# Split GELU and multiply in fp32: loads and stores trade queues, GELU in place, one instruction per tile

## The chip, the cores and the metric

The kernel runs on one core of a Trainium2 chip. The metric is the device time of one execution in microseconds (us), as a median over several runs. A profile is one execution, recorded with every instruction and every DMA packet. Its span is a little shorter than the measured time: the profiled execution of the kernel before shows a span of 469.1 us.

## The reference

```python
x: (32, 512, 2048) float32            # 134.22 MB in
x1, x2 = x[..., :1024], x[..., 1024:]
gelu_x1 = 0.5 * x1 * (1 + erf(x1 / np.sqrt(2)))
return (gelu_x1 * x2).astype(np.float32)   # 67.11 MB out
```

## The kernel before

The 16384 rows are cut into 16 tiles of 128 partitions x 8 rows. A tile's load is 8.39 MB, 64 KB a partition; its store is 4.19 MB, 32 KB a partition. There are two input tiles and two output tiles, so a load is two tiles ahead of the compute. ScalarE writes GELU of the left half into the output tile, VectorE multiplies it there by the right half. Middle tiles go in pieces of five and three rows; the first and the last tile in pieces of two, two and four.

```python
def load(i):
    x_tile = xpool.tile([P, R, dim], x.dtype, name="x_tile")      # bufs=2
    ... nc.sync.dma_start(out=x_tile[:, rows, :], in_=x_t[i][:, rows, :])

steps = ((0, 2), (2, 4), (4, 8)) if pieces else ((0, 5), (5, 8))
for lo, hi in steps:
    ... nc.scalar.activation(out=o_tile[:, rows, :], in_=x_tile[:, rows, :half], func=GELU)
    mul = nc.vector.tensor_mul(out=o_tile[:, rows, :], in0=o_tile[:, rows, :],
                               in1=x_tile[:, rows, half:])
...
if not pieces:
    store(nc.sync if i == n_tiles - 2 else nc.scalar, i, o_tile, slice(0, R))
if i + 2 < n_tiles:
    ahead.append(load(i + 2))
```

Because GELU writes the output tile, it waits for two things: the load of its tile and the store of two tiles ago.

## Time and profile before

| | before |
|---|---|
| time, median of 3 runs | 470.53 us (470.52 to 470.63) |
| span of the profile | 469.1 us |
| VectorE busy, ScalarE busy | 140.5 us, 115.5 us |
| mean share of the 16 DMA engines, 1.8 to 468 us | 1.00 |
| one middle tile | 29.05 us |

The prediction below shows the lines that carry this. Two more views are of use later. The first is the table of DMA queues of the kernel before (queue and kind, packets, MB, share of the 16 engines' time). SyncE's queue is q1, ScalarE's is q10.

```profile
q1 hardware_dynamic: 2880, 142.61, 70.4%
q10 hardware_dynamic: 2160, 58.72, 29.0%
```

Time and bytes are in proportion (0.49% per MB on both), so neither queue is the slower one. The second is the timeline at tile 1: start, duration, engine, line, operation.

```profile
60.38 0.36 ACTq L54 DMA_DIRECT2D out_dram<-o_tile  x1
71.58 7.12 ACT L71 ACTIVATE o_tile<-x_tile 128x5120 f32<-128x5120 f32 x2 [17.37 <-DMA out_dram<-o_tile]
```

Tile 1's store is issued at 60.38 us, and the transfers already under way end at about 71.6 us, when the next GELU can start. I call this distance, 11.2 us here, the **lead**: how long before the running transfers land the next ones are queued. In the steady state it is 15.7 us.

### The profile page before, as it was taken

How to read it: one execution, taken by the hardware profiler on the slowest of the kernel's cores; microseconds unless marked ns; L12 is line 12 of the kernel's file. 1: busy time of each engine (PE TensorE's matmuls, PEld its weight loads, DVE VectorE, ACT ScalarE, POOL GpSimd, SP SyncE). 2: the span in 40 equal slices, each digit the busy share in tenths (PEclk: the TensorE clock that was granted, in tenths of full speed). 3: DMA queues.
4: the chain of work that ended last, by engine and by line, in shares of the span. 5: the costliest groups of instructions: out<-in, count | busy, mean ns of one | idle time of the engine just before them, and what ended most of it. 6: DMA issues, size and time to landing. Idle time of an engine off the chain costs nothing.

```text
span 469.1 us, 179 instructions
## 1 busy us (share of the span) xinstructions
DVE 140.5 (30%) x34; ACT 115.5 (25%) x35; POOL 0.2 (0%) x4
## 2 busy tenths in 40 slices
DVE  0330615206051160611506015070250702407042
ACT  1320606041060410605005050050601406014060
POOL 0000000000000000000000000000000000000000
DMA  8999999999999999999999999999999999999998
GB/s 358 447 447 447 414 391 492 402 402 447 492 402 402 447 469 425 402 441 408 492 402 425 425 492 402 402 447 486 408 402 444 455 441 402 441 408 486 408 406 355
DMA packets 5041, 201.34 MB, mean 429 GB/s; under 512 B 560, under 2 KB 560, under 8 KB 560
## 3 DMA queue, kind: packets, MB, share of 16 engines
q1 hardware_dynamic: 2880, 142.61, 70.4%
q10 hardware_dynamic: 2160, 58.72, 29.0%
q14 instruction: 1, 0.01, 0.0%
HBM read 134.22 MB, written 67.11 MB: 429 GB/s over the span
## 4 chain that ended last, share of the span: by engine, by line
DMA 75%; DVE 14%; ACT 8%; ACTq 0%; issue 0%; SPq 0%
DMA out_dram<-o_tile 66%; DVE o_tile L75 14%; DMA x_tile<-in_x_dram 10%; ACT o_tile L71 8%; ACTq L115 0%; SPq L49 0%
## 5 line engine op out<-in xcount | busy, mean ns | idle before, releaser
L75 DVE TENSOR_TENSOR o_tile<-o_tile,x_tile 128x5120 f32<-128x5120 f32 (+3 forms) x34 | 140.5, 4171 | 320.4 <-ACT o_tile L71 320.4
L71 ACT ACTIVATE o_tile<-x_tile 128x5120 f32<-128x5120 f32 (+3 forms) x34 | 114.3, 3407 | 340.1 <-DMA out_dram<-o_tile 302.4
L71 ACT ACT_TABLE_LOAD x1 | 1.3, 1283 | 0.7 <-PEq L104 0.7
L104 POOL MEMSET const-bfloat16-1.0<- 128x1 bf16 x1 | 0.1, 101 | 0.0
L104 POOL MEMSET const-uint8-127<- 128x1 uint8 x1 | 0.1, 101 | 0.0
L104 POOL MEMSET const-float32-0.0<- 128x1 f32 x1 | 0.1, 98 | 0.2 <-issue 0.2
L104 POOL MEMSET const-float32-1.0<- 128x1 f32 x1 | 0.1, 98 | 0.0
## 6 DMA issues: line engine op xcount, KB each, us to landing
out_dram<-o_tile ACTq DMA_DIRECT2D x13, 4096.0 KB, 44.8
x_tile<-in_x_dram SPq DMA_DIRECT2D x2, 4096.0 KB, 16.8
out_dram<-o_tile ACTq DMA_DIRECT2D x2, 2048.0 KB, 34.3
out_dram<-o_tile SPq DMA_DIRECT2D x1, 4096.0 KB, 25.2
out_dram<-o_tile SPq DMA_DIRECT2D x2, 2048.0 KB, 7.5
x_tile<-in_x_dram SPq DMA_DIRECT2D x15, 44.6
```

Source lines behind the costliest of these rows:

```text
L71: nc.scalar.activation(out=o_tile[:, rows, :], in_=x_tile[:, rows, :half], func=GELU)
L75: mul = nc.vector.tensor_mul(out=o_tile[:, rows, :], in0=o_tile[:, rows, :], in1=x_tile[:, rows, half:],)
L104: nc = _bacc.Bacc("TRN2", target_bir_lowering=False, num_devices=1)
```

## The change

The intent is to take ScalarE off the wait for stores: GELU is computed in place in the input tile, and only the multiply needs a free output tile. Loads go out from ScalarE's queue and stores from SyncE's, the middle tiles use one instruction per engine, and waits that others imply are dropped.

```diff
-            dma = nc.sync.dma_start(out=x_tile[:, rows, :], in_=x_t[i][:, rows, :])
+            dma = nc.scalar.dma_start(out=x_tile[:, rows, :], in_=x_t[i][:, rows, :])
...
-        steps = ((0, 2), (2, 4), (4, 8)) if pieces else ((0, 5), (5, 8))
+        steps = ((0, 2), (2, 4), (4, 8)) if pieces else ((0, 8),)
...
-                    out=o_tile[:, rows, :], in_=x_tile[:, rows, :half], func=GELU
+                    out=x_tile[:, rows, :half], in_=x_tile[:, rows, :half], func=GELU
...
-                in0=o_tile[:, rows, :],
+                in0=x_tile[:, rows, :half],
                 in1=x_tile[:, rows, half:],
...
-            for ins in before_gelu[i % 2]:
-                tc.declare_no_dep(mul.ins, ins, reason="ScalarE waited for it")
+            no_wait(mul.ins, loads[i] + x_users[i % 2] + o_users[i % 2])
...
-            store(nc.sync if i == n_tiles - 2 else nc.scalar, i, o_tile, slice(0, R))
+            nc.sync.dma_start(out=o_t[i], in_=o_tile)
```

## The prediction

> **What bounds the kernel now.** I read the page first: the span, the busy shares, the strip of DMA business and the bytes.
>
> ```profile
> span 469.1 us, 179 instructions
> DVE 140.5 (30%) x34; ACT 115.5 (25%) x35; POOL 0.2 (0%) x4
> DMA  8999999999999999999999999999999999999998
> HBM read 134.22 MB, written 67.11 MB: 429 GB/s over the span
> ```
>
> VectorE (DVE) works 30% of the span and ScalarE (ACT) 25%. The DMA strip shows 9 in every slice but the first and the last. That is business, not yet rate, so the second view was the table of busy time by stretch, with cuts at 1.8 us, at 468 us, and around ten periods of the steady state (from one tile's first GELU at 129.49 us to another's at 420.00 us). The columns are the stretch, its length, DVE, ACT and POOL busy, a clock that says nothing here, the mean share of the 16 DMA engines, and GB/s.
>
> ```profile
> 0.00:1.80 1.80, 0.00 (x0) 1.08 (x1) 0.20 (x4) 1.00 0.40 109
> 1.80:468.00 466.20, 140.48 (x34) 114.46 (x35) 0.00 (x0) 1.00 1.00 431
> 468.00:469.10 1.10, 0.00 (x0) 0.00 (x0) 0.00 (x0) 1.00 0.00 0
> 129.49:420.00 290.51, 87.60 (x20) 71.22 (x20) 0.00 (x0) 1.00 1.00 433
> ```
>
> All 16 DMA engines are full, share 1.00, for 466.2 us out of 469.1 (packets are booked at their start, hence some bytes in the first row). The bytes that the reference demands, 134.22 + 67.11 = 201.33 MB, in 466.2 us are 431.9 GB/s. Ten steady tiles take 290.51 us, 29.05 us each; a tile is 8.39 MB in and 4.19 MB out, 12.58 MB, and 12.58 MB / 29.05 us = 433 GB/s. The kernel is bound by the rate of its DMA engines. The span is 1.8 us of start, 466.2 us of transfer and 1.1 us of end.
>
> The chain of waits seems to say otherwise, and was the third view, with the sums of the waits beside it.
>
> ```profile
> DMA out_dram<-o_tile 66%; DVE o_tile L75 14%; DMA x_tile<-in_x_dram 10%; ACT o_tile L71 8%; ACTq L115 0%; SPq L49 0%
> ACT o_tile L71 <- DMA out_dram<-o_tile: 302.4, 14, 22.0
> out_dram<-o_tile ACTq DMA_DIRECT2D x13, 4096.0 KB, 44.8
> x_tile<-in_x_dram SPq DMA_DIRECT2D x15, 44.6
> ```
>
> The chain runs GELU, multiply, store, and back to the GELU two tiles on, which writes the same output buffer; 22% of it is compute, and ScalarE waits 302.4 us for stores, some 22 us for each of 14 tiles. But a store takes 44.8 us from issue to landing although its 4.19 MB need only 9.7 us at 433 GB/s: it waits behind, and shares the engines with, other transfers. A load takes 44.6 us as well. The two, issued together, land together. So a wait for the store is a wait for the DMA engines, and the load that the same GELU needs comes no earlier. One period of the timeline shows the slack:
>
> ```profile
> 390.95 7.12 ACT L71 ACTIVATE o_tile<-x_tile 128x5120 f32<-128x5120 f32 x2 [21.89 <-DMA out_dram<-o_tile]
> 395.45 8.76 DVE L75 TENSOR_TENSOR o_tile<-o_tile,x_tile 128x5120 f32<-128x5120 f32 x2 [20.25 <-ACT o_tile L71]
> 404.24 0.33 SPq L49 DMA_DIRECT2D x_tile<-in_x_dram  x1
> 404.25 0.36 ACTq L54 DMA_DIRECT2D out_dram<-o_tile  x1
> 420.00 7.12 ACT L71 ACTIVATE o_tile<-x_tile 128x5120 f32<-128x5120 f32 x2 [21.93 <-DMA out_dram<-o_tile]
> ```
>
> The new load and store are queued at 404.25 us, 13.3 us after the tile's data were there (390.95). The pair before them keeps the engines busy until about 420.0. The queues are therefore refilled 15.7 us before they would run dry. This lead is the number on which the prediction rests.
>
> **What the Trainium skill says.** "DMA: Bandwidth & Descriptors", section "Issuing engines are not separate DMA queues", says that DMAs issued by different engines share the same 16 DMA engines, and that several issuers save only issue time. The trace agrees: one issue is 0.33 or 0.36 us against 29 us of period. The same page, section "Queues, rings and completion order", says that each DMA engine takes turns between the queues that have work, packet by packet. If a packet is one partition's contiguous piece, 64 KB of a load (8.39 MB / 128) and 32 KB of a store, that gives loads twice the bytes of stores, which fits the equal landing times (44.6 and 44.8 us), whichever queue carries which. Its section "Where 436 GB/s comes from" has a ceiling of 435.2 GB/s; the trace's 433 is 99.5% of it. Fourth, "VectorE: DVE Perf Modes", section "The TRN2 errata — SBUF-src ops pay a fixed extra latency per instruction", has (N+151)/0.96 ns for an fp32 product of two tensors: 5491 ns for 5120 elements, where the trace has 5492.
>
> **The change part by part.** (a) Swapped queues. Loads now leave from ScalarE, stores from SyncE. The build has the three first loads ahead of the activation-table load on ScalarE, so the first transfer starts when it did; an issue there costs 0.36 us instead of 0.33, or 0.03 us once at the start. The table load (1.28 us) moves to about 2 us, while the first data are there only at 12.9 us. No byte and no packet size changes. Sum: 0.0 us.
>
> (b) Whole-tile instructions. The groups by shape give the costs:
>
> ```profile
> L75 DVE TENSOR_TENSOR o_tile<-o_tile,x_tile 128x5120 f32<-128x5120 f32 x14 | 76.9, 5492 | 279.9 <-ACT o_tile L71 279.9
> L71 ACT ACTIVATE o_tile<-x_tile 128x5120 f32<-128x5120 f32 x14 | 62.6, 4469 | 301.2 <-DMA out_dram<-o_tile 280.3 <-DMA x_tile<-in_x_dram 20.9
> L75 DVE TENSOR_TENSOR o_tile<-o_tile,x_tile 128x3072 f32<-128x3072 f32 x14 | 46.9, 3351 | 0.0
> L71 ACT ACTIVATE o_tile<-x_tile 128x3072 f32<-128x3072 f32 x14 | 38.5, 2747 | 0.0
> ```
>
> ScalarE: (4469 - 2747) / 2048 = 0.841 ns an element, so 2747 + 5120 x 0.841 = 7.05 us for 8192. VectorE: (5492 - 3351) / 2048 = 1.045 ns, so 3351 + 5120 x 1.045 = 8.70 us. Fourteen instructions fewer on each engine save 14 x 0.16 us of ScalarE and 14 x 0.14 us of VectorE, both idle most of the time. But nothing overlaps within a tile any more: 7.05 + 8.70 = 15.75 us from data to stored result, where it was 404.25 - 390.95 = 13.3. That is 2.5 us later in each of 14 tiles, 35 us if it were on the path. It is not: the lead falls from 15.7 to 13.2 us and stays far from zero. Sum: 0.0 us.
>
> (c) GELU in place. It no longer waits for the store of two tiles ago; the multiply does. That store lands together with the load, so GELU starts some 0.2 us earlier at most, and by the time it is done, 7 us later, the store has landed. ScalarE's 302 us under "store" become waits for loads and for the multiply, ahead of whose end it can't issue the next load. Sum: 0.0 us.
>
> (d) Dropped waits. They are implied by others, and instructions that wait only on what has long been done cost nothing visible here.
>
> The end is the one place where compute could show. In the timeline the last half store is issued at 460.9 us and lands at 468.2. Before it, from 449.0 on, there are 4.19 MB of tile 14 and 2.10 MB of the first half, 6.29 MB / 433 = 14.5 us, to 463.5: the engines have 2.6 us in hand when the last store joins. The last tile keeps its three pieces and their durations, so this holds.
>
> Sum: 1.8 + 466.2 + 1.1 = 469.1 us of span, and with the 1.4 us that the measured time has over the span (470.53 - 469.1), **470.5 us**.
>
> **The rivals.** First, **the chain is real** and the store wait falls away: faster. For it speak 302.4 us of waits and a chain that is 66% stores. Against it: share 1.00 and 433 GB/s. Even at the page's 435.2 GB/s the bytes need 201.33 / 435.2 = 462.6 us, which would give 466.9 us, 0.8% less. So 2% is not to be had.
>
> Second, **lost overlap within the tile**, or ScalarE held up by the multiply before it may issue a load: slower. With all of it on the path, 470.5 + 35 = 505.5 us. For it speaks that ScalarE now stands in front of each load. Against it: 13.2 us of lead. An in-place or strided operand would have to slow both engines by over 80% first (13.2 / 15.75).
>
> Third, **sharing shifts**: with stores all in one queue and loads in the other, another alternation could change the mean packet rate. Half a per cent of rate is 2.3 us, so 468 to 473 us; for the total to move, the packets themselves have to change speed, and nothing in the change touches them.
>
> **Range and chances.** The three runs before span 0.1 us, so the range is only the third rival at about a third of its size and a start or end off by half a microsecond: 469.8 to 471.6 us. Faster by over 2% contradicts the bytes: 0.01. Slower by over 2% (9.4 us) needs a stall I have not seen: 0.02. Within 2%: 0.97.
>
> **What would show it.** In the profile after: DMA share 1.00 and some 432 GB/s from about 1.8 to 468 us; a period of 29.05 us; GELU about 7.05 us and multiply about 8.70 us for 8192 elements; the idle time before GELU put down to loads, none to stores; load and store queued some 13 us before the next GELU; the chain's shares quite different at an equal span. The prediction is wrong if the DMA share dips periodically (second rival), if the steady rate leaves 433 GB/s by over 0.5% at share 1.00 (third), or if the first transfer starts later than 2 us.

## More of the kernel before

A run of one core has no second core to compare its clock with. One run of the kernel before (474.27 us) lies 0.75% above the median of the seven of its rounds.

## The result, and the profile after

| | before | after |
|---|---|---|
| median of 6 runs | 470.53 us (470.46 to 470.73) | 470.58 us (470.36 to 470.78) |
| ratio, 95% interval | | 1.0 (0.9987 to 1.0013) |
| span of the profile | 469.1 us | 468.8 us |

The two kernels take the same time.

The page of the kernel after, its lines on span, busy engines, DMA and bytes, and its chain of waits:

```profile
span 468.8 us, 150 instructions
DVE 139.5 (30%) x20; ACT 114.2 (24%) x21; POOL 0.2 (0%) x4
DMA  8999999999999999999999999999999999999998
HBM read 134.22 MB, written 67.11 MB: 429 GB/s over the span
DMA x_tile<-in_x_dram 72%; DVE o_tile L77 14%; ACT x_tile L72 12%; ACTq L119 0%; ACTq L58 0%
```

The DMA strip is the same, slice for slice. The chain is another one: where stores had 66% of it, loads have 72%. A chain of waits names what came last by a little; where two transfers land together, it names either.

The table of busy time by stretch, after (stretch, length, DVE, ACT and POOL busy, a clock, mean share of the 16 DMA engines, GB/s):

```profile
1.80:468.00 466.20, 139.53 (x20) 114.23 (x21) 0.00 (x0) 1.00 1.00 431
129.38:419.54 290.16, 86.93 (x10) 70.29 (x10) 0.00 (x0) 1.00 1.00 434
```

The DMA engines are full over the same stretch. (It was cut by hand at 1.8 and 468 us. From the start of the first data packet to the end of the last, the packet records have 466.1 us before and 465.8 us after.) Ten tiles take 290.16 us, 29.02 us each. The groups by shape and the waits, after:

```profile
L77 DVE TENSOR_TENSOR o_tile<-x_tile 128x8192 f32<-128x8192 f32 x14 | 121.7, 8693 | 283.0 <-ACT x_tile L72 283.0
L72 ACT ACTIVATE x_tile<-x_tile 128x8192 f32<-128x8192 f32 x14 | 98.4, 7029 | 302.0 <-DMA x_tile<-in_x_dram 302.0
...
ACT x_tile L72 <- DMA x_tile<-in_x_dram: 339.4, 17, 22.0
```

ScalarE waited 302.4 us for stores and 37.8 us for loads before the change; it now waits 339.4 us for loads. The wait has changed its name and kept its length. One period of the timeline, then tile 1, and the DMA issues with their time to landing:

```profile
390.50 7.03 ACT L72 ACTIVATE x_tile<-x_tile 128x8192 f32<-128x8192 f32 x1 [22.02 <-DMA x_tile<-in_x_dram]
397.57 8.69 DVE L77 TENSOR_TENSOR o_tile<-x_tile 128x8192 f32<-128x8192 f32 x1 [20.35 <-ACT x_tile L72]
406.29 0.37 ACTq L58 DMA_DIRECT2D x_tile<-in_x_dram  x1
419.54 7.03 ACT L72 ACTIVATE x_tile<-x_tile 128x8192 f32<-128x8192 f32 x1 [22.01 <-DMA x_tile<-in_x_dram]
...
62.95 0.36 ACTq L58 DMA_DIRECT2D x_tile<-in_x_dram  x1
71.39 7.03 ACT L72 ACTIVATE x_tile<-x_tile 128x8192 f32<-128x8192 f32 x1 [17.20 <-DMA x_tile<-in_x_dram]
...
out_dram<-o_tile SPq DMA_DIRECT2D x14, 4096.0 KB, 42.4
x_tile<-in_x_dram ACTq DMA_DIRECT2D x15, 42.2
```

The result of a tile comes 15.8 us after its data (406.29 - 390.50), where it took 13.3. The next transfers are queued that much later, and land at the same moment as before: the time from issue to landing fell from 44.8 and 44.6 us to 42.4 and 42.2. The steady lead is 419.54 - 406.29 = 13.25 us. At tile 1 it is smaller, 71.39 - 62.95 = 8.4 us, because less was queued at the start: the GELUs of tiles 1 and 2 are 24.2 us apart (47.16 and 71.39 us) instead of 29.0.

### The profile page after: what moved, and what is told of

The parts are those of the page before. It is cut to its first block, busy times and chain, and to the rows that moved or that the text cites. A ratio compares the mean times of both kernels' runs of the same rounds, so it can differ in the third digit from the quotient of the medians.

```text
span 468.8 us, 150 instructions
## 1 busy us (share of the span) xinstructions
DVE 139.5 (30%) x20; ACT 114.2 (24%) x21; POOL 0.2 (0%) x4
## 4 chain that ended last, share of the span: by engine, by line
DMA 72%; DVE 14%; ACT 12%; ACTq 1%; issue 0%
DMA x_tile<-in_x_dram 72%; DVE o_tile L77 14%; ACT x_tile L72 12%; ACTq L119 0%; ACTq L58 0%
## 5 line engine op out<-in xcount | busy, mean ns | idle before, releaser
L77 DVE TENSOR_TENSOR o_tile<-x_tile 128x8192 f32<-128x8192 f32 (+2 forms) x20 | 139.5, 6985 | 320.7 <-ACT x_tile L72 320.7
L72 ACT ACTIVATE x_tile<-x_tile 128x8192 f32<-128x8192 f32 (+2 forms) x20 | 113.0, 5662 | 339.4 <-DMA x_tile<-in_x_dram 339.4
## 6 DMA issues: line engine op xcount, KB each, us to landing
out_dram<-o_tile SPq DMA_DIRECT2D x14, 4096.0 KB, 42.4
x_tile<-in_x_dram ACTq DMA_DIRECT2D x15, 42.2
```

Of the source, the lines that this page charges most:

```text
L72: nc.scalar.activation(out=x_tile[:, rows, :half], in_=x_tile[:, rows, :half], func=GELU)
L77: mul = nc.vector.tensor_mul(out=o_tile[:, rows, :], in0=x_tile[:, rows, :half], in1=x_tile[:, rows, half:],)
```

## The experiments

My theory is that the rate of the DMA engines sets the time as long as the lead is long enough (the lead theory). Its rivals: the chain of waits is real (the chain theory); how transfers are shared between queues sets the rate, and effects cancelled (the sharing theory).

### Two parts alone: queues_only and whole_only

```diff
# queues_only, in the kernel before
-            dma = nc.sync.dma_start(out=x_tile[:, rows, :], ...)
+            dma = nc.scalar.dma_start(out=x_tile[:, rows, :], ...)
-                store(nc.sync if last else nc.scalar, i, ...)     # both calls of store
+                store(nc.sync, i, ...)
# whole_only, in the kernel before
-        steps = ... if pieces else ((0, 5), (5, 8))
+        steps = ... if pieces else ((0, 8),)
```

> The kernel before with the queues swapped and nothing else. Lead theory (the DMA engines' rate sets the time while the queues are refilled before they run dry): 470.5 us within 0.5, load and store of a pair still land together, about 44.7 us after issue. Sharing theory (which queue carries what shifts the rate, and two shifts cancelled in the whole change): off by 1 us or more.

> The kernel before with one GELU and one multiply for each of the 14 middle tiles, queues and buffers as they were. Lead theory: 470.5 us within 0.5 although each tile's result is 2.4 us later; the time from issue to landing shrinks by these 2.4 us, to about 42.3. Rival (lost overlap is on the path, and another part of the change gave it back): up to 35 us more.

queues_only took 470.59 us (470.51 to 470.72), whole_only 471.09 us (471.00 to 471.29), the kernel before 470.73 us on the same chip (470.47 to 474.27, 7 runs). The intervals of both ratios hold 1. DMA issues, first of queues_only, then of whole_only:

```profile
out_dram<-o_tile SPq DMA_DIRECT2D x14, 4096.0 KB, 44.6
x_tile<-in_x_dram ACTq DMA_DIRECT2D x15, 44.4
```

```profile
out_dram<-o_tile ACTq DMA_DIRECT2D x13, 4096.0 KB, 42.3
x_tile<-in_x_dram SPq DMA_DIRECT2D x15, 42.1
```

Swapping the queues leaves the landing times alone. Whole-tile instructions shorten them by 2.4 us: the later issue comes out of the time that a transfer waits in its queue. Each part is worth nothing by itself, so nothing cancelled between these two. whole_only may be a few tenths of a microsecond slower; the runs don't settle that.

### The rate against the buffers: half_stores and deep

half_stores leaves out half of the stores of the middle tiles (its result is wrong). deep has tiles of half the size and four of each buffer. Its first version left out two half stores and gave a wrong result (470.42 us with 2.10 MB missing); deep_mended is the correct one.

```diff
# half_stores, in the kernel after
-            nc.sync.dma_start(out=o_t[i], in_=o_tile)
+            nc.sync.dma_start(out=o_t[i][:, 0:4, :], in_=o_tile[:, 0:4, :])
# deep_mended, in the kernel after (pieces of the first and last tile halved too)
-    R = 8
+    R = 4
-    x_tiles, o_tiles: 2 each, load(i + 2) after tile i
+    x_tiles, o_tiles: 4 each, load(i + 4) after tile i
```

> The kernel after storing only the first four of eight rows in the 14 middle tiles; the result is wrong on purpose. Compute and the order of waits stay. Lead theory: 29.36 MB fewer, 171.97 MB at 431.9 GB/s is 398.2 us, with 4.3 us of start, end and launch 402.5 us (400 to 406). A period that the waits set would stay near 29 us and the time near 470.

> The kernel after with tiles of half the size and four of each buffer instead of two. Lead theory: more buffers cannot help, no transfer was missing; half-size packets cost a little, 470 to 473 us. Chain theory (buffers come free too late): faster by over 2 us.

> The half-size tiles with four buffers each, with the fault of the first version mended (it left out two half stores, 2.10 MB, so was 4.9 us short at 432 GB/s). Lead theory: no gain, 470 to 476 us; 470.4 + 4.9 = 475.3 if the omission counts in full. Chain theory: under 468 us.

half_stores took 406.39 us in one look. A middle tile took (361.57 - 216.48) / 6 = 24.18 us, and its 10.49 MB in that time are 434 GB/s, the rate of the full kernel. The period follows the bytes, with compute and the order of waits unchanged. The two rows that bound these six tiles:

```profile
216.48 7.03 ACT L72 ACTIVATE x_tile<-x_tile 128x8192 f32<-128x8192 f32 x1 [17.16 <-DMA x_tile<-in_x_dram]
361.57 7.03 ACT L72 ACTIVATE x_tile<-x_tile 128x8192 f32<-128x8192 f32 x1 [17.14 <-DMA x_tile<-in_x_dram]
```

The total is 3.9 us over the expected 402.5, just outside the range of 400 to 406. Part of that is in the table of stretches of half_stores:

```profile
1.80:385.00 383.20, 130.61 (x17) 107.02 (x18) 0.00 (x0) 1.00 1.00 432
385.00:391.00 6.00, 3.31 (x2) 5.25 (x3) 0.00 (x0) 1.00 0.82 350
391.00:394.00 3.00, 2.19 (x2) 1.96 (x1) 0.00 (x0) 1.00 0.41 175
```

With half a store behind the last load, the engines run out of work while the last tile is computed, at 391 to 394 us. The full kernels have a whole store to cover this.

deep_mended took 472.48 us (472.41 to 472.71), 0.4% more than the kernel before (ratio 1.0042, 1.0026 to 1.0059). More buffers gained nothing, where the chain theory wanted less than 468 us. Four half-size buffers hold no more bytes than two full ones, and fewer bytes shorten the waits in a chain too, so neither run rules the chain theory out by itself. The stronger evidence against it is in the runs with more compute in the chain: whole_only above, and after_s2 below.

### The lead used up: after_s2, after_s3, before_s3, after_s3_pieces

VectorE passes once (s2) or twice more (s3) over each middle tile's GELU result. A maximum of a tensor with itself changes no value, so results stay correct. It takes 8.69 us, as the multiply does.

```diff
# after_s2 (range 1) and after_s3 (range 2), in the kernel after
+            for _ in range(0 if pieces else 1):
+                g = x_tile[:, rows, :half]
+                more = nc.vector.tensor_max(out=g, in0=g, in1=g)
             mul = nc.vector.tensor_mul(
# before_s3: the same in the kernel before, range 2, on o_tile
# after_s3_pieces: after_s3 with
-        steps = ... else ((0, 8),)
+        steps = ... else ((0, 5), (5, 8))
```

> The kernel after with one more VectorE pass over each middle tile (a maximum of the GELU result with itself, result unchanged), ahead of the multiply: 8.7 us more on the way from data to store. Lead theory: the lead falls from 13.2 to about 4.5 us and is not used up: 470.5 us within 1. Chain theory: 14 x 8.7 = 122 us more.

> The same with two more passes: 7.03 + 3 x 8.69 = 33.1 us from data to store, more than the 29.05 us of transfer, and the lead is gone. Lead theory: the 14 middle tiles take 33.2 us each, the time is about 47 + 14 x 33.2 + 20 + 2 = 534 us (528 to 538), the DMA share falls below 0.9, and GELU waits for no load any more.

> The kernel before with the same two passes over each middle tile, in its two pieces. Lead theory: 4.48 + 3 x (5.49 + 3.35) = 31.0 us from data to store, so 31.0 to 31.4 us a tile, 500 to 512 us in all; with the lead gone the overlap within the tile, which the change gives up, shows as some 2 us a tile, 25 to 30 us between this and the kernel after with the same passes.

> The kernel after with the two passes, but the middle tiles again in pieces of five and three rows. If the whole-tile instructions are what costs there: as the kernel before with the same passes, within 3 us (500 to 512). If it is loads issued from ScalarE behind the multiply, or GELU in place: as the whole-tile version, 528 us or more.

| | time, one look | a middle tile |
|---|---|---|
| after_s2 | 488.54 us | 29.00 us |
| after_s3 | 558.70 us | 33.65 us |
| before_s3 | 515.11 us | 31.61 us |
| after_s3_pieces | 509.35 us | 31.39 us |

after_s2 missed its expected 470.5 by 18 us, though its middle tiles took what they should. Stretches of after_s2, and a row of its timeline:

```profile
66.00:72.00 6.00, 5.62 (x1) 0.00 (x0) 0.00 (x0) 1.00 0.61 262
190.81:422.82 232.01, 139.07 (x16) 56.23 (x8) 0.00 (x0) 1.00 1.00 434
451.00:465.00 14.00, 11.25 (x3) 7.22 (x3) 0.00 (x0) 1.00 0.00 0
...
453.75 17.43 DVE L82 TENSOR_TENSOR o_tile<-x_tile 128x2048 f32<-128x2048 f32 x4 [15.17 <-ACT x_tile L72]
```

It lost in two places. At tile 1 the lead was 8.4 us and the pass takes 8.7, so the engines ran dry ahead of 72 us; by the last tile the GELU was 3.3 us late (451.81 us against 448.55 in the kernel after). And at the end the engines stood still for 14 us. The row of the timeline shows why: four multiplies run from 453.75 on, after the last tile's GELU, and the build had put tile 14's among them, behind the last tile's first piece. That is a fault of my probe, not of the kernel after, whose instructions are in order. In after_s3 the same fault made VectorE wait 17.8 us, so its total, which missed the expected 528 to 538 us, is not usable, but its steady state is. The stretches of steady state in after_s3, after_s3_pieces and before_s3, one row each:

```profile
114.59:484.74 370.15, 286.83 (x33) 77.32 (x11) 0.00 (x0) 1.00 0.91 374
```

```profile
203.86:455.00 251.14, 208.80 (x48) 56.98 (x16) 0.00 (x0) 1.00 0.97 401
```

```profile
175.88:460.35 284.47, 234.89 (x54) 64.10 (x18) 0.00 (x0) 1.00 0.95 396
```

(370.15 / 11 = 33.65, 251.14 / 8 = 31.39, 284.47 / 9 = 31.61 us a tile.) The DMA share is below 1: the engines run dry between tiles, and the compute sets most of the period. Now the overlap that whole-tile instructions give up is on the path, at 33.65 - 31.39 = 2.3 us a tile. With the pieces back, the kernel after is no slower a tile than the kernel before. So, against the kernel before, the whole-tile instructions cost this; GELU in place and the loads on ScalarE's queue cost nothing as long as the pieces are there. In after_s3 the two act together. ScalarE waits 346.1 us for the multiply there, because the issue of the next load stands before the next GELU on it and waits for the multiply. By the medians a load had landed some 2 us before (80.53 + 32.1 = 112.6 us, against a GELU at 114.59). before_s3 was 3 us over its expected range, 31.6 us a tile for 31.4 at most. after_s3_pieces lay within 500 to 512 us, but 5.8 us under before_s3 where at most 3 were expected.

### One queue: one_queue and one_queue_s3

```diff
# one_queue, in the kernel after; the load is issued ahead of the store
-            dma = nc.scalar.dma_start(out=x_tile[:, rows, :], ...)
+            dma = nc.sync.dma_start(out=x_tile[:, rows, :], ...)
-        if not pieces:
-            nc.sync.dma_start(out=o_t[i], in_=o_tile)
         x_users[i % 2].extend(gelus + muls + loads[i])
         o_users[i % 2].extend(muls)
         if i + 2 < n_tiles:
             load(i + 2)
+        if not pieces:
+            nc.sync.dma_start(out=o_t[i], in_=o_tile)
# one_queue_s3: the same in after_s3
```

> The kernel after with all transfers on SyncE's queue, each load ahead of the store that is issued with it. Lead theory: one queue is worked off in order, so a load lands some 9.7 us (4.19 MB at 433 GB/s) before the store issued with it instead of together with it; GELU, which no longer needs the store, then starts some 9 us before the multiply may; the time stays 470.5 us within 1. Sharing theory (taking turns between two queues is what reaches 433 GB/s, or costs some of it): off by 2 us or more.

> The kernel after with the two more passes and all transfers on SyncE's queue, loads ahead of stores. Lead theory: a load lands early enough for GELU to run beside the multiply of the tile before, and ScalarE is not held up by issuing; the way from the later of the two landings to the store is then VectorE's 26.1 us, below 29.05, so the DMA engines bound it again after a start that loses some 8 us: 472 to 485 us. If GELU in place can't be used even so: 528 us or more, as with two queues.

one_queue took 474.94 us (474.90 to 475.65), ratio 1.008 (1.0042 to 1.0117). Its DMA issues, then its stretches from one GELU to another eleven tiles on, and at the end:

```profile
out_dram<-o_tile SPq DMA_DIRECT2D x14, 4096.0 KB, 49.2
x_tile<-in_x_dram SPq DMA_DIRECT2D x15, 40.0
```

```profile
120.81:443.12 322.31, 95.62 (x11) 77.32 (x12) 0.00 (x0) 1.00 1.00 433
467.00:473.10 6.10, 0.00 (x0) 0.00 (x0) 0.00 (x0) 1.00 0.28 121
```

A load now lands 9.2 us before the store issued with it, as expected (9.7). With two queues they land together because the engines take turns: at 384 to 393 us in the kernel after, the packet records show nearly all 16 engines on a load packet (64 KB, 2.42 us), then nearly all on a store packet (32 KB, 1.21 us), in turn. That is the turn-taking with loads at twice the bytes that the prediction supposed. This is why GELU gained nothing by not waiting for the store.

The time was not within 1 us, so the sharing theory has something in it for this layout. The last stretch shows where: the mean share is 0.28 over 6 us. In the packet records the engines stop between 466.4 and 470.1 us after the first data packet starts (which engine a packet is on I inferred from starts and ends), where in the kernel after all stop between 465.5 and 465.8. With one queue some engines fall behind, and a load has landed only when the slowest is done: the GELUs are 322.31 / 11 = 29.30 us apart although the share is 1.00. Why they fall behind, no run shows.

one_queue_s3 took 486.91 us, 2 us over its expected range, and 29.65 us a tile ((454.99 - 128.88) / 11), against 33.65 in after_s3 with the same passes. With compute this near the bound, loads that land first and go out from SyncE let GELU in place run beside the multiply of the tile before: the GELU at 426.02 us starts while the multiply from 420.19 on is running. The one queue, the order of issue and the freed ScalarE came together here, so their shares in the gain are not separated.

### A shorter lead once more: after_s2_from_2

```diff
# in the kernel after
+            for _ in range(1 if 2 <= i < n_tiles - 1 else 0):
+                g = x_tile[:, rows, :half]
+                more = tc.keep_in_program_order(nc.vector.tensor_max(out=g, in0=g, in1=g))
-            mul = nc.vector.tensor_mul(...)
+            mul = tc.keep_in_program_order(nc.vector.tensor_mul(...))
```

> The kernel after with one more VectorE pass over tiles 2 to 14 (tile 1, which had the smaller lead, is left alone), and VectorE's instructions kept in program order. In the first such probe the middle tiles still took 29.0 us each; it lost some 3 us because the DMA engines ran dry ahead of tile 1's load, and some 15 us at the end where the build had moved tile 14's multiply behind the last tile's first piece. Lead theory: with both taken away, 13 x 8.7 = 113 us more of serial work leave the time at 470.5 us within 1. Rival (the 18 us came from the steady state, its lead is smaller than read): 485 us or more.

It took 481.45 us (480.93 to 481.94), ratio 1.0231 (1.0216 to 1.0247): a miss for the lead theory as I had put it, and not the rival's 485 either. Of 113 us of added serial work 10.9 us came through. Both faults of after_s2 were gone. The stretch of the twelve tiles from 100.33 to 459.00 us:

```profile
100.33:459.00 358.67, 208.61 (x24) 84.35 (x12) 0.00 (x0) 1.00 1.00 421
```

The engines are full and move 421 GB/s instead of 434. The tiles took 29.01 to 30.84 us, 29.89 in the mean (358.67 / 12); twelve times the 0.87 us over 29.02 is 10.4 us. The packet records show the loads' 64 KB packets longer, 2.49 us in the mean where the kernel after has 2.42: 195 of 1920 took over 5% more than the median, against 16 in the kernel after. In this stretch the packets' time over the usual 2.42 us (loads) and 1.21 us (stores) sums to 9.2 us per engine, so longer packets are most of the 10.4 us. They bunch where one tile's transfers give way to the next's. At one such place (tile 4) 15 engines finished within half a microsecond, and one 1.5 us later. In after_s2, with the same lead of 4.4 us between 100 and 450 us, nothing of this is seen, and that ran on another chip. Why it happened here stays open: chip, order of start, or engines out of step.

## Why the prediction was right, point by point

- **The bound.** Step: full DMA engines for 466.2 us, 433 GB/s. Right: the engines are as full after, and the packets span 465.8 us for 466.1. half_stores fits it: fewer bytes shortened the period in proportion (24.18 us, 434 GB/s).
- **The chain is not the bound.** Right. Its main member went from stores to loads at an equal span. 2.5 us more in each tile's chain cost at most a few tenths of a microsecond in all (whole_only), and 8.7 us more cost nothing a tile in after_s2 (29.00 us) and 0.9 us a tile in after_s2_from_2. Four buffers of half the size instead of two gained nothing (472.48 us).
- **Part (a), swapped queues.** Right: 470.59 us alone. In the kernel after the table load moved to 2.10 us, and the first GELU started at 12.88 us (before: 12.91).
- **Part (b), whole-tile instructions.** Right in size and place: 7.03 and 8.69 us for the 7.05 and 8.70 worked out. The tile's result is 2.5 us later (15.79 against 13.30 us), hidden here; 2.3 us a tile appear in after_s3 once nothing hides it, partly through the second rival's other half: ScalarE held behind the multiply.
- **Part (c), GELU in place.** Right that nothing is gained. That this hangs on load and store landing together fits one_queue, which pulls the landings 9.2 us apart so that GELU starts without the store; a gain in time shows only in one_queue_s3. GELU in place was not tried alone. I had expected ScalarE's idle time to be put down partly to the multiply; the waits name only loads.
- **Part (d), dropped waits.** Not tried by itself; only the sum of all parts is measured.
- **The sum.** Right, with one small error in its last term: 1.4 us of time over span compared the profile with other runs. The profiled run itself took 470.87 us, so its excess is 1.8 us (470.87 - 469.1), and its span was some 0.3 us longer than that of the median run. The two slips cancel, which is luck, though of 0.3 us only. The after value, 470.58 us over a span of 468.8, agrees with 1.8.
- **The lead.** The steady 13.2 us came out as 13.25. But I took it for the smallest, and tile 1 has 8.4 us, where after_s2 ran the engines dry. And "far from zero" was the right test only for the lead the change left: at 4.4 us one probe was hidden in its steady state and another lost 0.9 us a tile.
- **Third rival, sharing.** Rightly given little for this change: nothing touched the packets. The run with a single queue shows that moving transfers between queues can cost time, nearly twice what I gave it (4.2 us on the kernel before's 470.73, for 2.3), though with another order of issue. Its load packets changed little (2.44 us in the mean for 2.42); the engines fell out of step, which I had not thought of.

## What to carry to other kernels

When all 16 DMA engines are full and the bytes are fixed, ask how long before the running transfers land the next are queued; a change that takes well under this away, or frees an engine that only waits for transfers, doesn't move the time. Read that lead at every tile, the first ones above all, and don't spend it to the last few microseconds. A wait that vanishes from the list has gained nothing if another one ends at the same moment.

## What the Trainium skill lacked or had wrong

- "DMA: Bandwidth & Descriptors", section "Issuing engines are not separate DMA queues": saves only issue time, by the page. Here all transfers on one queue took 0.8% longer (474.94 us, ratio 1.008) than with two, with the engines ending 3.7 us apart instead of 0.3, although an issue costs only 0.33 to 0.37 us. The order of issue differs too, so the queue alone isn't shown to be the cause.
- No page I read says that load and store issued together on two queues land together, and so hide which of them is waited for (44.6 and 44.8 us with two queues, 40.0 and 49.2 with one). It follows from turn-taking once the packets are known to be 64 and 32 KB here; the conclusion isn't drawn.
- No page I read says that the first packets after a dry queue are longer: in after_s3 nearly every tile's first load packet on each of the 16 engines took about 0.75 us more than the usual 2.42 us (in before_s3 some 1.2 to 1.4 us).
- "VectorE: DVE Perf Modes", section "The TRN2 errata — SBUF-src ops pay a fixed extra latency per instruction": its formula (N+151)/0.96 gives 8691 ns for 8192 elements, where the trace has 8693. The page gives it for an fp32 add and checks it at 512 and 2048 elements; here it holds for a product, and beyond these sizes.
